# Keys and values of the prompt's latent attention: stored whole in memory and split by GpSimd when a head is fetched, values two heads at a time

## The chip, the cores and the metric

The kernel runs on one core of a Trainium2 chip. The metric is the device time of one execution in microseconds; the time of a kernel is the median of several executions. The profile shows one execution: what each engine did and when, and the clock that TensorE was granted (1.00 is its upper level of 2.4 GHz, 0.50 its lower level of 1.2 GHz).

The engines are TensorE (PE; its weight loads are PEld), VectorE (DVE), ScalarE (ACT), GpSimd (POOL) and SyncE (SP), which issues most of the DMA transfers; GpSimd issues the others here.

## What is computed

The reference is one step of a streaming encoder with two layers, over 1024 tokens of a prompt and 128 of samples. Each layer projects the normalised input, runs three mixers (a latent attention, a differential attention, a recurrence), gates them and merges them. The change concerns the latent attention of the prompt:

```python
c_q = rms_norm(c_q, lp['mla_q_norm'])
q = jnp.einsum('btr,rn->btn', c_q, lp['mla_w_uq']).reshape(B, T, MLA_HEADS, MLA_NOPE + MLA_ROPE)
...
c_kv = rms_norm(c_kv, lp['mla_kv_norm'])
...
q_lat = jnp.einsum('bthd,chd->bthc', q_nope, lp['mla_w_uk'])
...
s = jnp.einsum('bthc,bsc->bhts', ql, ckv_all) + jnp.einsum('bthr,bsr->bhts', qr, krope_all)
s = jnp.where(chunk_visible(qp, k_pos)[None, None], s.astype(jnp.float32) * mla_scale, NEG_INF)
p = jax.nn.softmax(s, axis=-1).astype(ckv_all.dtype)
return jnp.einsum('bhts,bsc->bthc', p, ckv_all)
```

There are 8 heads; a head has 64 features without position, 32 with rotary position, and values 64 wide. For the prompt the kernel does it the other way about: it expands the latents to keys and values of every head, 512 numbers of each per token.

## The kernel before, in words

A product of two float32 matrices is made of three matmuls (`mm3`, L196 to L202): each operand is split into a high part (a cast to a shorter form) and a low part (the rest), and high·high, high·low and low·high are added in PSUM. `split` (L191) makes the two parts of a tile: ScalarE casts the high part (L193), VectorE subtracts it for the low part (L194).

`layer` runs its stages one after the other: the differential attention, `c_phase`, `mla`, `mla_s` (the samples), the merge. Through all of them runs a queue of **filler tasks**, `z_task` and `gate_task`: products that depend on nothing but the layer's input. A task loads 512 KB of weights (`gs`, one buffer; SyncE, L236), ScalarE casts them (`gh`, L237), GpSimd makes the low part (`gl`, L240, four instructions). Then come three groups of 24 matmuls of 128x384 into `z` or `pg`; ScalarE takes the tanh of each group into a buffer `th` (four of them, L637 and L662), and SyncE stores `th` to `z` or `ts` (L646, L663). A credit in microseconds says how much filler stands between the matmuls of a stage; a burst of it, `BURST[4]`, stands before head 0's scores. A scheduler orders each engine's instructions once, when the program is built, and an engine works strictly in that order.

`c_phase` (L374) projects and normalises the latents, then makes three kinds of features and stores them: queries (`qn`, `qr`), keys (`keys`, L406: 128 features by up to 384 tokens at a time, into `kn`) and values (`vals`, L417: 128 tokens at a time, into `vm`). Each result is split on its way from PSUM into a tile `f` that holds both parts (`half`, `FB` = 6 buffers), and SyncE stores the tile, so that memory holds high and low parts side by side.

`mla` (L938) takes the heads in turn. `head(h)` fetches a head by four DMAs that GpSimd issues: `kT<-kn` (L957), `qT<-qn` (L958), `qT<-qr` (L959), `V<-vm` (L960). There are two buffers each of `kT`, `qT` and `V`, and head h uses `kT` and `qT` number h mod 2, so a fetch for head h waits until the scores of head h-2 are made. A unit is a head and a quarter of its queries. `scores` makes a unit's products into `sc` or `scm`; `soft` takes the maximum on VectorE (L811, L813) and the exponential on ScalarE into `P` (L821); two units later `pv` transposes `P` (L838), splits it into `ph` and `pl`, multiplies with `V` (L845 to L864), and `halves` (L876, L877) puts the sum into `ot`. At the end `rows_out` transposes the reciprocals of the row sums and stores them.

`mla_s` (L1018) begins with the samples' queries: GpSimd clears a part of `qrp` (L1024) and issues `qTh<-qn` and `qTl<-qn` (L1035); TensorE transposes `uk` into `ut` (L1047) and multiplies with `qTh` and `qTl` into `qlt`. Everything further in `mla_s` follows from `qlt`.

Of the kernel before, what the change touches and what calls it, by code (L numbers as in the profile page):

```python
# [9 lines left out]
F32 = mybir.dt.float32  # L10
# [4 lines left out]
ALU = mybir.AluOpType  # L15
# [3 lines left out]
DM, SEQ, NB, TS, PAST = 1024, 1024, 8, 16, 512  # L19
T = SEQ + NB * TS  # L20
NT = T // 128
NPT = SEQ // 128
EPS = 1e-6
NEG = -1e30
H = 8
QR, KR, NOPE, ROPE, VD = 256, 128, 64, 32, 64
# [12 lines left out]
def rr(ap):  # L39
    return ap.bitcast(F32)  # L40


class Net:
# [8 lines left out]
    TAIL = ((2, 0), (2, 1), (2, 2), (3, 0), (3, 1), (2, 3), (3, 2), (2, 4), (3, 3), (2, 5), (3, 4), (2, 6), (3, 5), (2, 7), (3, 6), (3, 7), (2, 8), (3, 8))  # L52
    GROUPS = (1, 3, 5, 7, 8)
    NORM = (0, 0)
    FB = 6
    CE = (1, 2, 1, 1)
    PVY = ((2, 1), (3, 1))
    TURNED = (1, 2)
# [202 lines left out]
    def setup(self):  # L261
        nc, ctx = self.nc, self.ctx
        i = self.i
        self.cp = ctx.enter_context(self.tc.tile_pool(name="cp", bufs=1))
        self.small = ctx.enter_context(self.tc.tile_pool(name="small", bufs=6))
        self.mmp = ctx.enter_context(self.tc.tile_pool(name="mmp", bufs=2, space=PSUM))
        self.ptp = ctx.enter_context(self.tc.tile_pool(name="ptp", bufs=2, space=PSUM))
        self.pop = ctx.enter_context(self.tc.tile_pool(name="pop", bufs=1, space=PSUM))
        self.scp = ctx.enter_context(self.tc.tile_pool(name="scp", bufs=3, space=PSUM))
        c = self.cp  # L270
        self.ident = c.tile([128, 128], F32, name="ident")
        nc.sync.dma_start(self.ident, i["k_ident"])
        self.identr = c.tile([128, 128], F32R, name="identr")
        nc.vector.tensor_copy(self.identr, self.ident)
        self.ones = c.tile([128, 2], F32, name="ones")
        nc.vector.memset(self.ones, 1.0)
        self.e2 = c.tile([128, 2], F32, name="e2")
        self.xpool = ctx.enter_context(self.tc.tile_pool(name="xpool", bufs=1))
        self.xh = self.xpool.tile([128, 8, T], F32R, name="xh")
        self.xl = self.xpool.tile([128, 8, T], F32R, name="xl")  # L280
        dt = self.tc.dram_tile
        ls = range(self.depth)
        self.qn = [dt([H * NOPE, 2, T], F32, name=f"qn{l}") for l in ls]
        self.qr = [dt([H * ROPE, 2, T], F32, name=f"qr{l}") for l in ls]
        self.kn = [dt([H * NOPE, 2, SEQ], F32, name=f"kn{l}") for l in ls]
        self.kr = [dt([ROPE, 2, T], F32, name=f"kr{l}") for l in ls]
        self.vm = [dt([H, 128, NPT, 2, VD], F32, name=f"vm{l}") for l in ls]
        self.qf, self.kf = ([[dt([512, T], F32, name=f"{k}{l}{x}") for x in "hl"] for l in ls] for k in ("qf", "kf"))
        if self.only == "debug":
            self.ob = [[self.o[f"ob{l}_{b}"] for b in range(3)] for l in range(self.depth)]  # L290
        else:
            self.ob = [[dt([512, T], F32, name=f"ob{l}_{b}") for b in range(3)] for l in range(self.depth)]
        self.zscr = [[dt([512, T], F32, name=f"z{l}_{b}") for b in range(2)] for l in range(self.depth)]
        self.hscr = [dt([LW, T], F32, name=f"hscr{l}") for l in range(self.depth)]
        self.rscr = [[dt([8, T], F32, name=f"rs{l}_{b}") for b in range(2)] for l in range(self.depth)]
        self.tscr = {(l, b): dt([DM, T], F32, name=f"ts{l}_{b}") for l in range(self.depth) for b in self.SPILL}
        self.xscr = dt([T, DM], F32, name="xscr")
# [76 lines left out]
    def c_phase(self, l):  # L374

        nc, i, o = self.nc, self.i, self.o
# [5 lines left out]
        with self.pool("cph") as p, ExitStack() as ea:  # L382
# [17 lines left out]
            def half():  # L400
                return pb.tile([128, 2, 384], F32R, tag="f", name="f", bufs=self.FB)

            def spill(dst, row, n, t0, x, tn=384):
                nc.sync.dma_start(dst[l][row : row + n, :, t0 : t0 + tn], rr(x[:n, :, :tn]))

            def keys(t0, tn):  # L406

                for b in range(4):
                    ps = self.sc()[:, :tn]
                    bs, ts = slice(b * 128, b * 128 + 128), slice(t0, t0 + tn)  # L410
                    self.mm3(ps, [(kvh[:, 0, bs], kvl[:, 0, bs], self.ckTh[:, ts], self.ckTl[:, ts])])
                    x = half()
                    self.split(ps, x[:, 0, :tn], x[:, 1, :tn])
                    spill(self.kn, b * 128, 128, t0, x, tn)
                    yield 0.5

            def vals(t):  # L417

                ps = self.sc()
                ts = slice(t * 128, t * 128 + 128)  # L420
                self.mm3(ps, [(self.ckTh[:, ts], self.ckTl[:, ts], kvh[:, 1], kvl[:, 1])])
                for g in range(2):
                    x = half().rearrange("p x t -> p (x t)")[:, :512].rearrange("p (h x v) -> p h x v", h=4, x=2)
                    self.split(ps[:, g * 256 : g * 256 + 256].rearrange("p (h v) -> p h v", h=4), x[:, :, 0], x[:, :, 1])
                    nc.sync.dma_start(self.vm[l][g * 4 : g * 4 + 4, :, t].rearrange("h p x v -> p h (x v)"), rr(x).rearrange("p h x v -> p h (x v)"))
                yield 0.65

            def project(t, raws):
# [46 lines left out]
            pb = ea.enter_context(self.pool("cpb"))  # L475
# [5 lines left out]
            for k in range(2):  # L481
                sv = st[:, k].rearrange("p (h d) -> p h d", d=96)
                for d0, d1, c0 in ((0, 64, 0), (64, 96, 512)):
                    hv, lv = (x[:, k, c0 : c0 + 8 * (d1 - d0)].rearrange("p (h d) -> p h d", h=8) for x in (uh, ul))
# [12 lines left out]
            for t in range(NT):  # L497
                ps = self.sc()[:, :256]
# [7 lines left out]
                c, t0 = t // 3, (t - 2) * 128  # L506

                for b in range(4):
                    ps = self.sc()[:, :384]
                    yield from self.proj_n(ps, t0, 384, uh, ul, kch=2, n0=b * 128, xh=cqh, xl=cql)  # L510
                    x = half()
# [3 lines left out]
                for b in range(2):  # L515
                    ps = self.pt("qrt")[:, :384]
                    for k in range(3):
                        nc.tensor.transpose(ps[:, k * 128 : k * 128 + 128], qs[k][:, b * 4 : b * 4 + 4].rearrange("p h r -> p (h r)"), self.ident)
                    x = half()
# [3 lines left out]
                ps = self.pt("krt")[:, :384]  # L523
                for k in range(3):
                    nc.tensor.transpose(ps[:32, k * 128 : k * 128 + 128], krn[:, t - 2 + k], self.ident)
                x = half()
                self.split(ps[:32], x[:32, 0], x[:32, 1])
                pn = min(SEQ - t0, 384)
                spill(self.kr, 0, ROPE, t0, x)
                yield  # L530
                yield from keys(t0, pn)
                for k in range(t - 2, min(t + 1, NPT)):
                    yield from vals(k)
# [404 lines left out]
    def mla(self, l):  # L938
        nc, i = self.nc, self.i
        with self.pool("mla") as p:  # L940
# [2 lines left out]
            nc.vector.memset(mask[0:64, 448:512], NEG)  # L943
            lsum = p.tile([128, NPT, H, 2], F32, name="lsum")
            nc.vector.memset(lsum, 0.0)
            ops, Ps = {}, {}
            kTs, qTs = ([p.tile([128, 2, SEQ], F32R, name=f"{x}T{k}") for k in range(2)] for x in "kq")
            for kT in kTs:
                nc.gpsimd.dma_start(kT[64:96], self.kr[l][:, :, :SEQ])
# [3 lines left out]
            def head(h):  # L953

                kT, qT = kTs[h % 2], qTs[h % 2]
                V = p.tile([128, NPT, 2 * VD], F32R, tag="V", name="V", bufs=2)
                nc.gpsimd.dma_start(kT[:64], self.kn[l][h * 64 : h * 64 + 64])  # L957
                nc.gpsimd.dma_start(qT[:64], self.qn[l][h * 64 : h * 64 + 64, :, :SEQ])  # L958
                nc.gpsimd.dma_start(qT[64:96], self.qr[l][h * 32 : h * 32 + 32, :, :SEQ])  # L959
                nc.gpsimd.dma_start(V, self.vm[l][h].rearrange("p t x v -> p t (x v)"))  # L960
                ops[h] = qT, kT, V
                yield

# [21 lines left out]
            def values(u):  # L985
# [11 lines left out]
                yield  # L997

            self.pipeline([(h, g) for h in range(H) for g in range(4)], lambda u: (u[0], lambda: head(u[0])), prep, scores, values, 4, self.BURST[4], self.LAG[1], (lambda u: (2 * (2 + (u[1] > 1)), self.pv_steps(1, u[1]))) if self.SPREAD[1] else None, self.WIDE)
            rl = p.tile([128, NPT * H], F32, name="rlm")  # L1000
            nc.vector.tensor_reduce(rl, lsum.rearrange("p i h k -> p (i h) k"), axis=AX.X, op=ALU.add)
            nc.vector.reciprocal(rl, rl)
            self.rows_out(p, rl, NPT, self.rscr[l][0], 0)

    def rows_out(self, p, r, nt, dst, t0):

        nc = self.nc
        for k0 in range(0, nt, 2):
            m = min(2, nt - k0)
            ps = self.pt("rst")  # L1010
            for t in range(m):
                nc.tensor.transpose(ps[:8, t * 128 : t * 128 + 128], r[:, (k0 + t) * 8 : (k0 + t) * 8 + 8], self.ident)
            ro = p.tile([8, 256], F32, tag="ro", name="ro", bufs=1)
            nc.scalar.copy(ro[:, : m * 128], ps[:8, : m * 128])
            nc.sync.dma_start(dst[:, t0 + k0 * 128 : t0 + (k0 + m) * 128], ro[:, : m * 128])

# [707 lines left out]
```

## Time and profile before

| | us |
|---|---|
| median of 3 runs | 3026.06 (3023.16 to 3031.2) |
| the profiled execution's own time | 3023.51 |
| its span in the trace | 3021.6 |
| TensorE busy in the span | 2857.7 (95%) |
| VectorE, ScalarE, GpSimd busy | 1651.7, 1395.0, 772.8 |
| bytes read and written in memory | 265.89 MB and 127.66 MB |
| `c_phase` of layer 0, its dense part | 886 to 934 |
| scores of `mla`, layer 0 | 957 to 1099 |
| mean granted clock | 0.987 |

Times in the rows further down are microseconds from the span's start. "Busy" leaves out register, branch, semaphore and DMA-issuing instructions. An engine's idle time is put down to what released it: `[3.58 <-ACT th L662]` reads: idle for 3.58 us, until ScalarE's write of `th` on line 662 was done. The time of an execution and its span differ by what lies before and behind the traced instructions (here 1.9 us).

### The profile page before, as it was taken

To read this page: it belongs to the slowest core of one execution; us is meant where nothing else is said; L and a number is where in the kernel's file an instruction comes from. 1 tells how busy PE (TensorE), PEld (TensorE's weight loads), DVE (VectorE), ACT (ScalarE), POOL (GpSimd) and SP (SyncE) were. 2 spreads that over 40 slices of the span, in tenths; PEclk is the share of its full clock that TensorE was granted. 3 is DMA by queue.
4 is the path that set the end of the run, shared out by engine and by line. 5 is a ranking of instruction groups with operands and counts; after the bars stand their busy time and mean duration, and the time that the engine had idled before them with its cause. 6 is when DMAs were issued, how large, how long until landed. Compare 5 with 4: busy or idle time off the path is not lost. (4 is left out here: it accounts for less than half of the span.)

```text
span 3021.6 us, 50750 instructions
## 1 busy us (share of the span) xinstructions
PE 2857.7 (95%) x18466; PEld 2705.9 (90%) x18466; DVE 1651.7 (55%) x3947; ACT 1395.0 (46%) x3367; POOL 772.8 (26%) x1132
## 2 busy tenths in 40 slices
PE   7999999999998999999989999999999989999998
PEld 7899899999897888999989998999999978889998
DVE  6322878747255855555343328777561557545543
ACT  4433766646333765312234347666452447542121
POOL 2221335120102113352131313342101111133620
PEclk9999999999999999999999999999999999999999
DMA  5434545265248533764133345452642584427541
GB/s 168 129 98 106 125 111 140 69 180 164 75 124 246 123 81 84 220 184 162 63 116 125 92 116 126 113 142 64 190 141 79 161 215 119 95 76 231 171 156 73
DMA packets 387658, 396.89 MB, mean 131 GB/s; under 512 B 56192, under 2 KB 342496, under 8 KB 386344
## 3 DMA queue, kind: packets, MB, share of 16 engines
q1 hardware_dynamic: 368048, 331.70, 36.7%
q0 software_dynamic: 19360, 61.95, 9.2%
q8 instruction: 146, 2.39, 0.3%
q14 instruction: 104, 0.85, 0.1%
HBM read 265.89 MB, written 127.66 MB: 130 GB/s over the span
## 5 line engine op out<-in xcount | busy, mean ns | idle before, releaser
L200 PE MATMUL pg<-xh,gh 128*128 128x384 f32 x1152 | 401.2, 348 | 7.5 <-ACT th L662 7.5
L821 ACT ACTIVATE P<-sc,mx 128x384 f32<-128x384 f32 (+4 forms) x598 | 335.5, 566 | 130.7 <-DVE mx L811 100.2
L201 PE MATMUL pg<-xl,gh 128*128 128x384 f32 x1152 | 395.8, 344 | 0.0
L202 PE MATMUL pg<-xh,gl 128*128 128x384 f32 x1152 | 395.3, 343 | 0.0
L240 POOL TENSOR_TENSOR gl<-gs,gh 128x256 fp32r<-128x256 f32 x288 | 230.3, 829 | 585.8 <-ACT gh L237 527.3
L194 DVE TENSOR_TENSOR pl<-pt,ph 128x512 fp32r<-128x512 f32 (+1 forms) x320 | 199.6, 634 | 53.2 <-ACT ph L193 50.8
L200 PEld LDWEIGHTS pg<-xh,gh 128*128 128x128 f32 x1152 | 218.2, 189 | 11.4 <-ACT th L662 9.2
L201 PEld LDWEIGHTS pg<-xl,gh 128*128 128x128 f32 x1152 | 218.1, 189 | 2.7
L202 PEld LDWEIGHTS pg<-xh,gl 128*128 128x128 f32 x1152 | 218.1, 189 | 0.9
L193 ACT CAST ph<-pt 128x512 fp32r<-128x512 f32 (+1 forms) x320 | 169.5, 544 | 81.8 <-PE pt L845 80.1
L200 PE MATMUL z<-xh,gh 128*128 128x384 f32 x576 | 203.3, 353 | 0.0
L201 PE MATMUL z<-xl,gh 128*128 128x384 f32 x576 | 199.6, 346 | 0.0
L202 PE MATMUL z<-xh,gl 128*128 128x384 f32 x576 | 198.4, 344 | 0.0
L200 PE MATMUL sc<-wyh,xh 128*128 128x256 f32 x576 | 163.0, 283 | 5.8 <-DVE xt L1550 5.8
L200 PE MATMUL dp<-wh,xh 128*128 128x256 f32 x576 | 165.2, 287 | 3.4 <-ACT e L575 2.1
L201 PE MATMUL dp<-wl,xh 128*128 128x256 f32 x576 | 164.4, 285 | 0.8 <-POOL wl L555 0.8
L202 PE MATMUL dp<-wh,xl 128*128 128x256 f32 x576 | 164.3, 285 | 0.0
L202 PE MATMUL sc<-wyh,ml 128*128 128x256 f32 x576 | 162.9, 283 | 0.0
L201 PE MATMUL sc<-wyl,xh 128*128 128x256 f32 x576 | 162.9, 283 | 0.0
L1235 PE MATMUL sc<-kT,qT 98*128 98x384 f32 (+3 forms) x384 | 140.6, 375 | 5.2 <-ACT P L821 4.6
L240 POOL TENSOR_TENSOR wol<-wos,woh 128x128 fp32r<-128x128 f32 x192 | 101.0, 554 | 172.2 <-ACT woh L237 153.6
L813 DVE TENSOR_REDUCE mx<-sc 128x1 f32<-128x384 f32 (+2 forms) x200 | 116.0, 586 | 39.1 <-PE sc L202 21.0
(456 smaller groups left out, 8355.3 us busy)
## 6 DMA issues: line engine op xcount, KB each, us to landing
gs<-in_w_in_dram SPq DMA_DIRECT2D x72, 512.0 KB
ts<-th SPq DMA_DIRECT2D x144, 192.0 KB
th<-ts SPq DMA_DIRECT2D x144, 192.0 KB
K<-in_cache_diff_k_dram SPq DMA_DIRECT2D x64, 256.0 KB
Vt<-in_cache_diff_v_dram SPq DMA_DIRECT2D x32, 512.0 KB
u<-ob SPq DMA_DIRECT2D x48, 288.0 KB
ws<-in_w_in_dram SPq DMA_DIRECT2D x24, 512.0 KB
z<-th SPq DMA_DIRECT2D x48, 192.0 KB
```

The source lines that it names most:

```text
L193: nc.scalar.copy(hi, src)
L194: (lo_engine or nc.vector).tensor_tensor(lo, src, rr(hi), op=ALU.subtract)
L200: nc.tensor.matmul(out, ah, bh, start=start and k == 0, stop=False)
L201: nc.tensor.matmul(out, ah, bl, start=False, stop=False)
L202: nc.tensor.matmul(out, al, bh, start=False, stop=stop and k == n - 1)
L240: (lo_engine or nc.gpsimd).tensor_tensor(lo[:, k : k + half], st[:, k : k + half], rr(hi[:, k : k + half]), op=ALU.subtract)
L813: nc.vector.tensor_reduce(mx, sc[:, : n1 - n0], axis=AX.X, op=ALU.max, negate=True)
L821: nc.scalar.activation(P[:, n0:n1], scs[k][:, : n1 - n0], AF.Exp, bias=mx, scale=1.0 if adds[k] is None else -1.0, accum_out=l2[:, k : k + 1])
L1235: nc.tensor.matmul(ps, lhs, kT[:, m, n0:n1], start=True, stop=True)
```

## The change

`kn` and `vm` hold whole float32 numbers, half the bytes. In `c_phase` a key tile and a value tile are copied from PSUM by one instruction, on ScalarE and VectorE by turns, into buffers of their own, `kx` (three) and `vx` (two); a value tile is stored by one DMA in place of two. `f` is left to the queries and the rotary keys and has 4 buffers. In `mla`, `head(h)` fetches the whole keys into a tile `kx` (one buffer), and every other head the whole values of two heads into `vx` (one buffer). In a second step the two parts are made from them: on GpSimd, a copy and a subtraction each for keys and values, and for head 0 on ScalarE and VectorE by `split`. `rows_out` uses two buffers under another name.

```diff
-    FB = 6
+    FB = 4
...
-        self.kn = [dt([H * NOPE, 2, SEQ], F32, name=f"kn{l}") for l in ls]
+        self.kn = [dt([H * NOPE, SEQ], F32, name=f"kn{l}") for l in ls]
...
-        self.vm = [dt([H, 128, NPT, 2, VD], F32, name=f"vm{l}") for l in ls]
+        self.vm = [dt([SEQ, H * VD], F32, name=f"vm{l}") for l in ls]
...
-                    x = half()
-                    self.split(ps, x[:, 0, :tn], x[:, 1, :tn])
-                    spill(self.kn, b * 128, 128, t0, x, tn)
+                    x = pb.tile([128, 384], F32, tag="kx", name="kx", bufs=3)
+                    (nc.vector.tensor_copy if b % 2 else nc.scalar.copy)(x[:, :tn], ps)
+                    nc.sync.dma_start(self.kn[l][b * 128 : b * 128 + 128, ts], x[:, :tn])
...
-                for g in range(2):
-                    x = half().rearrange("p x t -> p (x t)")[:, :512].rearrange("p (h x v) -> p h x v", h=4, x=2)
-                    self.split(ps[:, g * 256 : g * 256 + 256].rearrange("p (h v) -> p h v", h=4), x[:, :, 0], x[:, :, 1])
-                    nc.sync.dma_start(self.vm[l][g * 4 : g * 4 + 4, :, t].rearrange("h p x v -> p h (x v)"), rr(x).rearrange("p h x v -> p h (x v)"))
+                x = pb.tile([128, 512], F32, tag="vx", name="vx", bufs=2)
+                (nc.vector.tensor_copy if t % 2 else nc.scalar.copy)(x, ps)
+                nc.sync.dma_start(self.vm[l][ts], x)
...
-                nc.gpsimd.dma_start(kT[:64], self.kn[l][h * 64 : h * 64 + 64])
+                kx = p.tile([64, SEQ], F32, tag="kx", name="kx", bufs=1)
+                nc.gpsimd.dma_start(kx, self.kn[l][h * 64 : h * 64 + 64])
                 nc.gpsimd.dma_start(qT[:64], self.qn[l][h * 64 : h * 64 + 64, :, :SEQ])
                 nc.gpsimd.dma_start(qT[64:96], self.qr[l][h * 32 : h * 32 + 32, :, :SEQ])
-                nc.gpsimd.dma_start(V, self.vm[l][h].rearrange("p t x v -> p t (x v)"))
+                if h % 2 == 0:
+                    vx[0] = p.tile([128, NPT, 2 * VD], F32, tag="vx", name="vx", bufs=1)
+                    nc.gpsimd.dma_start(vx[0], self.vm[l][:, h * 64 : h * 64 + 128].rearrange("(t p) v -> p t v", p=128))
+                yield
+
+                vs = vx[0][:, :, h % 2 * VD : h % 2 * VD + VD]
+                for src, hi, lo in ((kx, kT[:64, 0], kT[:64, 1]), (vs, V[:, :, :VD], V[:, :, VD:])):
+                    if h:
+                        nc.gpsimd.tensor_copy(hi, src)
+                        nc.gpsimd.tensor_tensor(lo, src, rr(hi), op=ALU.subtract)
+                    else:
+                        self.split(src, hi, lo)
                 ops[h] = qT, kT, V
...
-            self.rows_out(p, rl, NPT, self.rscr[l][0], 0)
+            self.rows_out(p, rl, NPT, self.rscr[l][0], 0, "hv", 2)
```

The scheduler's order moves with it, in three places. The first is GpSimd's order in the middle of the heads. Before, a head is four DMAs:

```order
L957 DMA kT_10477<-kn_91 64x2048
L958 DMA qT_10479<-qn_87 64x2x1024
L959 DMA qT_10479<-qr_89 32x2x1024
L960 DMA V<-vm_95 128x1024
L957 DMA kT_10477<-kn_91 64x2048
```

Now (a head of even number, then one of odd number, which fetches no values):

```order
L968 CAST kT_10424<-kx 64x1024
L969 TENSOR_TENSOR kT_10424<-kx,kT_10424 64x1024
L957 DMA kx<-kn_91 64x1024
L968 CAST V<-vx 128x8x64
L958 DMA qT_10427<-qn_87 64x2x1024
L969 TENSOR_TENSOR V<-vx,V 128x8x64
L959 DMA qT_10427<-qr_89 32x2x1024
L968 CAST kT_10425<-kx 64x1024
L969 TENSOR_TENSOR kT_10425<-kx,kT_10425 64x1024
```

The split of a head and the fetch of the next stand between one another: the fetch of `kx` comes behind the split of the keys, the fetches of the queries behind parts of the split of the values.

The second place is GpSimd's order from the last head into `mla_s`. Before (`qrp`, `qTh` and `qTl` are those of `mla_s`, `gl` is a filler task's):

```order
L960 DMA V<-vm_95 128x1024
L1024 MEMSET qrp 32x1024
L1035 DMA qTh<-qn_87 64x8x128
L1035 DMA qTl<-qn_87 64x8x128
L240 TENSOR_TENSOR gl<-gs,gh 128x256 x4
```

Now:

```order
L968 CAST V<-vx 128x8x64
L969 TENSOR_TENSOR V<-vx,V 128x8x64
L240 TENSOR_TENSOR gl<-gs,gh 128x256 x4
L1035 MEMSET qrp 32x1024
L1046 DMA qTh<-qn_87 64x8x128
L1046 DMA qTl<-qn_87 64x8x128
```

The four `gl`, which wait for ScalarE's `gh`, moved from behind the fetches for `mla_s` to ahead of them.

The third place is ScalarE's order at the entry to `mla`. Before (`gh` are filler weights, the `P` are head 0's first units):

```order
L662 ACTIVATE th<-pg 128x384
L237 CAST gh<-gs 128x1024
L662 ACTIVATE th<-pg 128x384 x2
L821 ACTIVATE P,lsum<-sc,mx 128x128
L821 ACTIVATE P,lsum<-sc,mx 128x256
L821 ACTIVATE P,lsum<-sc,mx 128x384
L237 CAST gh<-gs 128x1024
L821 ACTIVATE P,lsum<-sc,mx 128x512
```

Now:

```order
L237 CAST gh<-gs 128x1024
L636 ACTIVATE th<-z 128x384 x3
L237 CAST gh<-gs 128x1024
L636 ACTIVATE th<-z 128x384
L193 CAST kT_10424<-kx 64x1024
L661 ACTIVATE th<-pg 128x384 x2
L820 ACTIVATE P,lsum<-sc,mx 128x128
L193 CAST V<-vx 128x8x64
L820 ACTIVATE P,lsum<-sc,mx 128x256
L820 ACTIVATE P,lsum<-sc,mx 128x384
L820 ACTIVATE P,lsum<-sc,mx 128x512
```

The CAST of `gh` that stood ahead of the unit's last `P` is gone from this place (it stands among the `P` of head 1 now), and head 0's two CASTs stand ahead of its first and its second `P`. Lines of the changed kernel lie 1 lower from `c_phase` on, and 11 higher behind `head`.

## Rows read from the trace of the kernel before

**Rows 1.** The page: busy time, share of the span and instructions of each engine.

```profile
PE 2857.7 (95%) x18466; PEld 2705.9 (90%) x18466; DVE 1651.7 (55%) x3947; ACT 1395.0 (46%) x3367; POOL 772.8 (26%) x1132
```

**Rows 2.** Windows: stretch, its length, busy (count) per engine, clock, DMA share, GB/s.

```profile
886.00:934.00 48.00, 48.00 (x288) 45.13 (x287) 33.01 (x84) 24.01 (x57) 2.84 (x4) 1.00 0.92 304
934.00:957.00 23.00, 19.42 (x101) 18.97 (x100) 10.71 (x14) 4.46 (x10) 6.85 (x12) 0.93 0.98 269
957.00:979.00 22.00, 11.94 (x60) 10.08 (x59) 8.77 (x23) 10.01 (x29) 4.08 (x8) 0.77 0.60 137
979.00:1099.00 120.00, 112.97 (x772) 98.74 (x770) 95.82 (x234) 92.78 (x262) 13.75 (x25) 1.00 0.47 107
...
2436.00:2459.00 23.00, 19.60 (x104) 19.15 (x102) 10.62 (x14) 4.47 (x11) 7.24 (x13) 0.93 0.97 260
2459.00:2481.00 22.00, 11.52 (x58) 9.68 (x57) 8.70 (x23) 9.87 (x30) 3.73 (x7) 0.77 0.60 138
```

**Rows 3.** Waits, 880 to 1140 us: engine, line, releaser; total us, times, longest.

```profile
PE sc L200 <- ACT P L821: 9.2, 1, 9.2
...
PE pg L200 <- ACT th L662: 3.6, 1, 3.6
```

**Rows 4.** Timeline of ScalarE: start, us, instruction, idle time before it and releaser.

```profile
950.69 0.49 ACT L662 ACTIVATE th<-pg 128x384 f32<-128x384 f32 x1 [10.72 <-DMA z<-th]
...
969.07 1.04 ACT L237 CAST gh<-gs 128x1024 fp32r<-128x1024 f32 x1 [9.24 <-DMA gs<-in_w_in_dram]
...
1121.45 1.05 ACT L237 CAST gh<-gs 128x1024 fp32r<-128x1024 f32 x1 [2.23 <-PE pg L201]
```

**Rows 5.** DMA issues, 880 to 1100 us: count, KB each, median us to landing.

```profile
kT<-kn POOLq DMA_DIRECT2D x8, 512.0 KB, 6.8
...
V<-vm POOLq DMA_DIRECT2D x8, 512.0 KB, 4.9
...
qTh<-qn POOLq DMA_DIRECT2D x1, 256.0 KB, 4.2
```

**Rows 6.** GpSimd's groups by form: busy, mean ns, idle time before.

```profile
L240 POOL TENSOR_TENSOR gl<-gs,gh 128x256 fp32r<-128x256 f32 x288 | 230.3, 829 | 585.8 <-ACT gh L237 527.3 <-PE kst L1360 41.8 <-PE ckt L1086 16.6
...
L1216 POOL TENSOR_TENSOR V<-nat,V 128x512 fp32r<-128x512 f32 x16 | 20.6, 1285 | 21.1 <-ACT V L1215 21.0
```

**Rows 7.** Timeline of GpSimd in the heads.

```profile
977.99 2.82 POOL L240 TENSOR_TENSOR gl<-gs,gh 128x256 fp32r<-128x256 f32 x4
...
1010.80 0.57 POOL L960 DMA_DIRECT2D V<-vm  x1 [15.40 <-PE sc L202]
...
1028.27 0.57 POOL L960 DMA_DIRECT2D V<-vm  x1 [15.25 <-PE scm L202]
```

**Rows 8.** Timeline of GpSimd at the end of `mla`.

```profile
1098.71 0.95 POOL L1024 MEMSET qrp<- 32x1024 f32 x1 [17.01 <-PE sc L202]
1099.61 0.69 POOL L1035 DMA_DIRECT2D qTh<-qn  x1
...
1122.64 2.81 POOL L240 TENSOR_TENSOR gl<-gs,gh 128x256 fp32r<-128x256 f32 x4 [21.66 <-ACT gh L237]
```

**Rows 9.** Timeline of TensorE: the first `qlt` product.

```profile
1126.77 0.32 PE L200 MATMUL qlt<-qTh,uTh 64*128 64x128 f32 x1
```

**Rows 10.** Windows: a hole elsewhere in the span and the 3 us behind it.

```profile
1262.00:1266.00 4.00, 1.21 (x7) 0.92 (x7) 3.94 (x5) 0.62 (x1) 4.00 (x3) 0.97 0.73 215
1266.00:1269.00 3.00, 3.00 (x11) 3.00 (x10) 1.60 (x3) 0.67 (x1) 2.65 (x5) 0.50 0.26 71
```

**Rows 11.** Waits, 884 to 936 us: ScalarE for the stores from `f`.

```profile
ACT f L193 <- DMA qn<-f: 1.6, 3, 0.7
...
ACT f L193 <- DMA qr<-f: 1.0, 2, 0.6
```

**Rows 12.** Timeline of VectorE, beside the `gl` of rows 7.

```profile
979.52 1.18 DVE L194 TENSOR_TENSOR pl<-pt,ph 128x384 fp32r<-128x384 f32 x2 [1.22 <-ACT ph L193]
```

**Rows 13.** VectorE's group of that form over the whole span: busy, mean ns.

```profile
L194 DVE TENSOR_TENSOR pl<-pt,ph 128x384 fp32r<-128x384 f32 x128 | 70.7, 553 | 23.7 <-ACT ph L193 23.0
```

More of the change, by code (lines that the diff above doesn't have):

```diff
@@ L945, in mla @@
             nc.vector.memset(lsum, 0.0)
-            ops, Ps = {}, {}
+            ops, Ps, vx = {}, {}, [None]
             kTs, qTs = ([p.tile([128, 2, SEQ], F32R, name=f"{x}T{k}") for k in range(2)] for x in "kq")
@@ L1002, in mla, with rows_out @@
             nc.vector.reciprocal(rl, rl)
-            self.rows_out(p, rl, NPT, self.rscr[l][0], 0)
-    def rows_out(self, p, r, nt, dst, t0):
+            self.rows_out(p, rl, NPT, self.rscr[l][0], 0, "hv", 2)
+    def rows_out(self, p, r, nt, dst, t0, tag="ro", bufs=1):
         nc = self.nc
@@ L1012, in rows_out @@
                 nc.tensor.transpose(ps[:8, t * 128 : t * 128 + 128], r[:, (k0 + t) * 8 : (k0 + t) * 8 + 8], self.ident)
-            ro = p.tile([8, 256], F32, tag="ro", name="ro", bufs=1)
+            ro = p.tile([8, 256], F32, tag=tag, name="ro", bufs=bufs)
             nc.scalar.copy(ro[:, : m * 128], ps[:8, : m * 128])
```

## The prediction, made before the changed kernel ran

> **What bounds the kernel now.** The page's busy times come first: TensorE is busy for 95% of the span and no other engine for more than 55% [rows 1]. So an edit pays only where TensorE waits or runs slowly, and the next view is the table of windows around the code that changes [rows 2]. In `c_phase` (886 to 934 us) TensorE is busy for 48.00 of 48 us at full clock, while the DMA engines are busy for 0.92 of the time: they are nearly full, but nothing waits for them yet. The bill comes at the entry to `mla`. From 934 to 957 us TensorE lacks 3.58 us and its mean clock is 0.93; from 957 to 979 us it lacks 10.06 us at 0.77. Then the heads run well: 112.97 busy of 120 us at clock 1.00. Layer 1 shows the same at 2436 and 2459 us.
>
> The list of waits names the two holes: 3.6 us behind ScalarE's `th`, 9.2 us behind ScalarE's `P` [rows 3]. ScalarE's timeline tells what it stood on [rows 4]. At 950.69 us the tanh into `th` had waited 10.72 us for a buffer that the store `z<-th` had not yet read out, so here the full DMA engines reach TensorE. At 969.07 us a CAST for a filler task's weights (`gh`) had waited 9.24 us for its load, and the last `P` of head 0's first unit stood behind it in ScalarE's order. A hole costs more than its length, since the clock is at half speed after it: 0.07 of 19.42 busy us is 1.4 us, 0.23 of 11.94 is 2.7 us. Layer 0 loses 3.6 + 1.4 + 9.2 + 2.7 = 16.9 us. Layer 1, by its windows and with the same 0.86 us of small gaps taken off the second, loses 3.4 + 1.4 + 9.6 + 2.7 = 17.1 us. Together **34.0 us** can be won, 1.1% of the time.
>
> **The change part by part.** *Bytes.* The eight key fetches and eight value fetches of a layer are 512 KB each [rows 5], so `kn` and `vm` are 4.2 MB each, written and read. Halved, 4.2 MB fewer are written in a stretch that moves 304 GB/s: 13.8 us of transfer per layer. A backlog of about ten us at the end of `c_phase` is what held `z<-th` back, so the first hole (3.6 + 1.4) should close. It also lets the first heads' fetches land earlier, and in `mla`, where the DMA engines are busy for 0.47, it frees what nobody waits for.
>
> *Order at the entry.* By the order of instructions the CAST of `gh` that blocked `P` now stands some 20 instructions later, among those of head 1. So the second hole (9.2 + 2.7) should go too. In its place ScalarE and VectorE split head 0's keys and values: CAST `kT` stands ahead of two `th` and the first `P`, CAST `V` ahead of the second `P`. They wait for the fetches `kx` and `vx`, which wait for the stores of the last chunk. Counting matmuls, 141 of the filler stand between the last `vals` product and head 0's first scores; they were 95. At 48.00/288 = 0.17 to 0.18 us each that is about 25 us. The way from the last store through the fetches is two landings: with 6.8 us [rows 5] for a fetch and up to twice that in full queues, plus about 3 us for the two splits, I get 17 to 25 us. So it fits barely; I take 1 us per layer left over, between 0 and 5.
>
> *The split on GpSimd.* For each head from 1 on, four instructions: CAST and subtraction for 64x1024 of `kT`, and the same for 128x512 of `V`. Subtractions of 128x256 take 829 ns and of 128x512 1285 ns [rows 6], so 1.8 ns for a further element and 2.2 us for 1024. The two subtractions are 1.29 + 2.2 = 3.5 us. No row has a CAST of this size on GpSimd; between nothing and the subtractions' price, that is 0 to 3.5 us. It walks as many elements, so I take 2.8, nearer the upper end: 6.3 us per head (3.5 to 7.0). GpSimd has room: it issues four DMAs per head of 0.5 to 0.6 us and then stands idle for over 15 us of 17.5, as before the `V` fetch at 1010.80 us [rows 7]. A head's `kT` may be written when the scores of the head two before it are done, 17.5 us before it is needed; 6.3 us of split and some 2 us of issues end well within that. The fetch of queries now stands behind two CASTs and a subtraction, some 5 us later, with 10 us left to land. I cost the split at nothing. Its cover is this idle time; without it every head would be longer, which is a rival below. ScalarE and VectorE lose 16 instructions each per layer, off the path.
>
> *The end of `mla`.* Here the change adds a wait. Before, GpSimd cleared `qrp` and issued `qTh` and `qTl` at 1099.61 us, 27 us before the first `qlt` product that reads them; the four `gl` came at 1122.64 us [rows 8, 9]. Now the four `gl` stand ahead, and they wait for ScalarE's CAST of `gh` (1121.45 us in the trace [rows 4]). From that CAST's start t: the `gl` start at t+1.2 and end at t+4.0, the memset of 0.95 ends at t+4.95, `qTh` is issued there and lands 4.2 us later [rows 5], at t+9.15; `qTl` 0.7 us after. The product wants it at 1126.77 - 1121.45 = 5.3 us, and 5 more filler matmuls stand ahead of it now, so t+6.2. The hole is 2.9 us (to 3.6 if `qTl` counts). Behind the wait stand the two fetches alone, but the whole of `mla_s` follows from `qlt`. After a hole of 2.8 us elsewhere the clock is at half for 3 us [rows 10], 1.5 us lost. Sum 4.4 us per layer, **+8.8**; at least +5.8 without the clock, at most +10.2.
>
> *Buffers in `c_phase`.* With 4 `f` instead of 6, a buffer comes round sooner, but keys and values no longer use it. ScalarE already waits for stores from `f`: 1.6 us in three and 1.0 us in two [rows 11], and TensorE shows none of it. Bounds: 0 (TensorE's 48.00 of 48) to 6 us per layer (half of the 21 `f` tiles that are left, at 0.6). I take three waits of 0.7, **2 us** per layer, as the densest stretch keeps its order.
>
> Sum from the profiled execution's own 3023.5 us: -34.0 + 8.8 + 4 (`f`) + 2 (entry) = -19.2, so 3004.3 us. The median of the runs is 2.5 us above that execution; I say **3005 us**.
>
> **Rivals.** *The wait moves within `c_phase`* (3011 us). Four buffers and stores that stay near the DMA limit (0.92) give back 5 us per layer instead of 2. For it: `f` is already waited for. Against: fewer tiles share the buffers.
>
> *The entry hole is only halved* (3019 us). If the chain of store, fetch and split takes 25 us plus 7 (one further landing of 6.8), head 0's scores stand 7 us in each layer instead of 1, with a half clock of 1.4 behind: +15. For it: two landings in a row under a DMA share of 0.98. Against: 13.8 us fewer of transfer ahead of it. This is also how the change would look if halved bytes relieve nothing.
>
> *Nothing is lost at the end* (2993 us). If the CAST of `gh` comes earlier than the products need, the +8.8 falls away, and `f` costs 1.
>
> *GpSimd and VectorE hold each other up* (3043 us, slower). If each of GpSimd's splits keeps VectorE from working, VectorE's 95.82/120 x 17.5 = 14.0 us per head become 20.3, 2.8 over the head's 17.5: 14 heads make +39. It decides as soon as more than 3.5 us per head collide. Against: at 979.52 us VectorE made two subtractions in 1.18 us, beside the `gl` of 977.99 us that ran till 980.8: 0.59 us each, where the mean is 0.55 [rows 7, 12, 13]. The Trainium skill (SBUF — State Buffer, "SBUF: two separate sides") says that VectorE and GpSimd share a port pair as an exclusive lock, held for a whole instruction, when VectorE reads two SBUF operands. By that rule this case stays small, since those subtractions, and VectorE's other work in the heads, read one operand from PSUM; the trace agrees. The skill also advises against the move as such: in GPSIMD Engine Reference, "Engine selection", two-input elementwise work on GpSimd is put at about twice VectorE's time. By these rows it is 1.285 us for 512 columns against 0.55 us for 384, so about 1.75; it changes the sum only where GpSimd is waited for.
>
> **How the numbers follow.** My case has 0.48 (3000 to 3010), the `f` waits 0.15, the halved hole 0.19, nothing lost at the end 0.10, the collision 0.08. This kernel's measurement can tell about 0.3% or 9 us from no change: faster is below 3017, slower above 3035. So faster has 0.48 + 0.15 + 0.10 = 0.73, same 0.19, slower 0.08. The range goes from 2993 to 3022: it takes in all but the collision and the worse half of the halved hole.
>
> **What would show it.** Right: no hole behind `th` or `P` at the entry and clock 1.00 there; the fetches `kT<-kn` gone, `kx` of 256 KB; a hole of about 3 us ahead of `qlt`, with `qTh` issued behind four `gl`; heads still 17.5 us apart, GpSimd busy 6 to 9 us in each; DMA share in `c_phase` clearly under 0.92. Wrong: heads longer than 17.5 us; a wait for `kT` or `V` by the scores of any head after the first; a hole of several us at head 0; `f` waits on TensorE in `c_phase`.

## The result, and the profile after

The changed kernel takes 3012.25 us in the median (8 runs, 3005.64 to 3016.94), the kernel before 3024.61 us (8 runs, 3020.65 to 3031.2). The ratio is 0.9949 with a 95% interval of 0.9936 to 0.9961: 0.5% faster, some 15 us by the ratio and 12.4 us between these medians, where 3005 us was forecast with a range of 2993 to 3022. The time lies in the range, but 7 us above the figure and outside the main case's 3000 to 3010; the gain is two thirds to four fifths of the 19.2 us in the forecast's sum. The profiled execution took 3012.3 us with a span of 3010.5 us.

The page's busy times (columns as in [rows 1]):

```profile
PE 2862.9 (95%) x18466; PEld 2708.3 (90%) x18466; DVE 1650.8 (55%) x3915; ACT 1386.3 (46%) x3335; POOL 847.4 (28%) x1180
```

TensorE does the same matmuls and is busy for 5.2 us more than in [rows 1]: the span fell by 11.1 us, so its idle time fell by 16.3 us, and a part of that was given back at half clock. The table of windows says where (columns as in [rows 2]); here `mla` begins at about 955 us:

```profile
886.00:934.00 48.00, 47.51 (x282) 43.00 (x281) 31.12 (x74) 21.00 (x46) 2.48 (x5) 1.00 0.78 270
934.00:957.00 23.00, 21.87 (x125) 21.27 (x124) 12.84 (x18) 6.11 (x14) 11.57 (x17) 1.00 0.93 205
957.00:969.00 12.00, 11.51 (x66) 9.57 (x65) 7.82 (x22) 8.55 (x28) 7.33 (x7) 1.00 0.71 162
969.00:1089.00 120.00, 113.59 (x775) 98.85 (x774) 96.90 (x234) 94.18 (x262) 43.59 (x44) 1.00 0.31 76
...
1112.00:1119.00 7.00, 4.49 (x27) 3.88 (x25) 0.68 (x1) 1.07 (x2) 4.17 (x6) 0.98 0.87 222
1119.00:1133.00 14.00, 13.23 (x51) 12.37 (x52) 3.23 (x7) 2.75 (x5) 3.61 (x12) 0.52 0.51 103
1133.00:1140.00 7.00, 6.99 (x52) 6.35 (x49) 5.38 (x20) 4.33 (x13) 2.76 (x8) 1.00 0.48 114
```

The DMA share in `c_phase` fell from 0.92 to 0.78. At the entry TensorE now lacks 1.13 us of 23 and 0.49 of 12, at clock 1.00, where [rows 2] had 3.58 and 10.06 at 0.93 and 0.77. The heads run as before, with GpSimd busy for 43.59 us of 120 and no longer 13.75. And behind the heads stands a stretch that was not there: TensorE is busy for 13.23 of 14 us, but at clock 0.52, so that 51 matmuls fit where the 7 us behind it hold 52.

TensorE's waits from 880 to 1000 us, longest first, answer to [rows 3]; both of its rows are gone:

```profile
PE po L859 <- ACT ph L193: 1.4, 3, 0.6
PE pg L200 <- DVE th L638: 1.1, 1, 1.1
PE sc L200 <- ACT P L820: 0.5, 2, 0.2
```

The end of `mla` answers to [rows 8, 9]. GpSimd's timeline:

```profile
1111.04 2.82 POOL L240 TENSOR_TENSOR gl<-gs,gh 128x256 fp32r<-128x256 f32 x4 [39.39 <-ACT gh L237]
1113.92 0.95 POOL L1035 MEMSET qrp<- 32x1024 f32 x1
1114.82 0.73 POOL L1046 DMA_DIRECT2D qTh<-qn  x1
1115.54 0.68 POOL L1046 DMA_DIRECT2D qTl<-qn  x1
```

TensorE's timeline there, the first `qlt` product and the place where the clock came back:

```profile
1119.57 0.44 PE L200 MATMUL qlt<-qTh,uTh 64*128 64x128 f32 x1 [2.73 <-DMA qTh<-qn]
...
1131.91 0.52 PE L200 MATMUL pg<-xh,gh 128*128 128x384 f32 x1
1132.23 0.44 PE L201 MATMUL pg<-xl,gh 128*128 128x384 f32 x1
1132.50 0.34 PE L202 MATMUL pg<-xh,gl 128*128 128x384 f32 x1
```

GpSimd had stood idle for 39 us, waiting for `gh` with the fetches behind it. The hole is 2.73 us; a filler matmul takes 0.52 us and not 0.34 until 1132.2 us.

To price the places, count TensorE's matmuls (18466 in either trace) and compare the times at which each trace reaches the same count. From count 5400 to 6400 lies the entry of layer 0, from 6400 to 7200 the end of its `mla`; 14800, 15700 and 16600 bound the same places in layer 1. The changed kernel's two profiled executions (the first two rows) differ by up to 2 us at one place, so less than that says nothing. Microseconds gained (-) or lost (+) against the kernel before:

| kernel | entry 0 | end 0 | entry 1 | end 1 |
|---|---|---|---|---|
| changed | -14.3 | +8.0 | -15.3 | +8.2 |
| changed, once more (e10) | -16.3 | +7.7 | -15.6 | +8.3 |
| e1, `qTh` by SyncE | -16.0 | +0.3 | -15.3 | +2.7 |
| e3, stores twice | -8.2 | +8.5 | -5.5 | +8.4 |
| e5, fetches of before in bytes | -16.1 | +7.2 | -17.2 | +8.7 |
| e6, both | -6.6 | +7.7 | -5.6 | +8.5 |
| e9, before with later fetches | -6.8 | -0.1 | -7.3 | +0.3 |

The entries give 29.6 us, the ends take back 16.2.

### The profile page after: what moved, and what is told of

It reads as the page before. It is cut to its first block, busy times and chain, and to the rows that moved or that the text cites. A ratio compares the mean times of both kernels' runs of the same rounds, so it can differ in the third digit from the quotient of the medians.

```text
span 3010.5 us, 50598 instructions
## 1 busy us (share of the span) xinstructions
PE 2862.9 (95%) x18466; PEld 2708.3 (90%) x18466; DVE 1650.8 (55%) x3915; ACT 1386.3 (46%) x3335; POOL 847.4 (28%) x1180
## 5 line engine op out<-in xcount | busy, mean ns | idle before, releaser
L237 ACT CAST gh<-gs 128x1024 fp32r<-128x1024 f32 x72 | 75.7, 1052 | 120.4 <-DMA gs<-in_w_in_dram 37.9
```

Source lines behind the costliest of these rows:

```text
L237: nc.scalar.copy(hi, st)
```

## The experiments

The runs were made on chips on which the kernel before took 3030.9, 3030.5 and 3032.9 us in the median, more than the 3024.61 us above. So what is compared is the ratio to the kernel before on the same chip.

### e1 and e11: the fetches of `mla_s` out of GpSimd's queue

```diff
-                    nc.gpsimd.dma_start(qT[x], self.qn[l][:, x, SEQ:].rearrange("(h d) t -> d h t", h=H))
+                    nc.sync.dma_start(rr(qT[x]), self.qn[l][:, x, SEQ:].rearrange("(h d) t -> d h t", h=H))
```

> The changed kernel with qTh and qTl fetched by SyncE in place of GpSimd, so that they no longer stand behind the four gl; TensorE's order stays as in the changed kernel up to there. Theory A (at the end of mla the wait for the fetches costs a hole of 2.7 to 3.0 us and, behind it, some 6 us of half clock, 8 to 9 us in each layer): the hole is at most 1 us, the granted clock stays 1.00 behind it, and the time falls by 17 us, 12 to 19, to about 2995. Theory B (the hole alone costs; the clock falls there in any case, because of the narrow qlt products): the time falls by 6 us to about 3006 and the clock is still 0.5 for some 13 us behind the first qlt.

The ratio is 0.9909 (0.9891 to 0.9926). The changed kernel, 0.9949, is 0.0040 above it: 12 us, the lower end of theory A. Windows of e1 from 1115 us on, around its first `qlt` products:

```profile
1115.00:1122.00 7.00, 6.46 (x38) 5.81 (x37) 0.68 (x1) 2.15 (x4) 3.78 (x5) 1.00 0.68 159
1122.00:1136.00 14.00, 13.98 (x98) 12.96 (x98) 7.55 (x21) 7.28 (x18) 6.77 (x18) 1.00 0.71 170
```

and its first `qlt` product:

```profile
1121.59 0.29 PE L200 MATMUL qlt<-qTh,uTh 64*128 64x128 f32 x1 [0.35 <-DMA qTh<-qn]
```

The hole is 0.35 us, and the 14 us behind it hold 98 matmuls at clock 1.00 where the changed kernel's 14 us held 51 at 0.52. The same narrow products run, so in layer 0 they are not what brings the clock down (theory B falls there): the hole is. By the table the two ends cost 0.3 and 2.7 us now, so 13.2 us were won there. In layer 1 a window of 14 us behind the products still has clock 0.88, with no wait of TensorE over 1.1 us near it; why is open.

The same kernel again, with the changed kernel beside it:

> The version of e1 once more, beside the changed kernel on the same chip: by the 8.4 and 9.7 us that the two tails cost, less 1 us left in each, 0.004 to 0.006 below the changed kernel's ratio (theory A of e1); 0.002 or less below it if the clock's part of these were not to be won.

> The changed kernel as it is, once more, beside the two others of this call on one chip: the ratio to the kernel before stays within 0.9936 to 0.9961 if chips and days do not matter at this level.

e11's ratio is 0.9906 (0.9889 to 0.9922), e10's 0.9952 (0.9936 to 0.9969): 0.0046 apart, as theory A had it. This version beats both kernels, by 0.9% and 0.45%.

### e2: work in the hole

```diff
+                    if h4 == 0:
+                        dm = self.pt("dm")
+                        for k in range(26):
+                            nc.tensor.matmul(dm[:, :384], self.xh[:, k % 8, :128], self.xh[:, k % 8, :384], start=k == 0, stop=k == 25)
                     ps = self.pt("qlt")
```

> The changed kernel with 26 further matmuls of 128x384, whose result nobody reads, ahead of the first qlt product of each layer: 26 x 0.174 = 4.5 us of work per layer, and the fetches come as late as before. Theory A (the hole brings the clock down): no hole, clock 1.00 behind it, per layer +4.5 of work, -2.9 of hole, -6 of half clock: -4.4, so about 9 us less in all, near 3003. Theory B (the clock falls there in any case): +1.6 per layer, so 3 us more, near 3015, with the clock at 0.5 behind the qlt products.

The ratio is 0.9962 (0.9947 to 0.9976), 4 us above the changed kernel: theory B's number, but not its reason. TensorE's timeline:

```profile
1110.07 4.78 PE L1064 MATMUL dm<-xh 128*128 128x384 f32 x26
1115.14 0.29 PE L200 MATMUL qlt<-qTh,uTh 64*128 64x128 f32 x1 [0.29 <-DMA qTh<-qn]
1117.64 0.47 PE L201 MATMUL qlt<-qTl,uTh 64*128 64x128 f32 x1 [2.21 <-DMA qTl<-qn]
```

The scheduler also moved filler matmuls: 13 that stood ahead of the product with `qTl` in the changed kernel stand behind it now, so that TensorE met that second fetch 2.21 us early. A hole was left, and the clock fell behind it again. The run therefore does not separate the theories (e1 does); it shows that a hole of 2.2 us is enough here.

### e3: the bytes of the stores back

```diff
+                    nc.sync.dma_start(self.kn2[l][b * 128 : b * 128 + 128, ts], x[:, :tn])
                     nc.sync.dma_start(self.kn[l][b * 128 : b * 128 + 128, ts], x[:, :tn])
...
+                nc.sync.dma_start(self.vm2[l][ts], x)
                 nc.sync.dma_start(self.vm[l][ts], x)
```

> The changed kernel with each store of keys and values made twice, the second copy into a memory tensor that nobody reads: the writes of c_phase are as many bytes as before the change. The scheduler then puts the CAST of gh back ahead of head 0's last P. Theory A (the gain at the entry to mla comes from the bytes written in c_phase, through the store z<-th, the load gs and the order that follows from them): the holes come back, 20 to 34 us more than the changed kernel, 3032 to 3046. Theory B (the gain comes from the whole layout: fewer splits in c_phase, or GpSimd's splits): at most 5 us more.

The ratio is 1.0005 (0.999 to 1.002), 17 us above the changed kernel. That is 3 us short of theory A and far from B; what it shows is in the parts. Its waits from 880 to 1140 us:

```profile
ACT th L665 <- DMA z<-th: 9.2, 1, 9.2
PE qlt L200 <- DMA qTh<-qn: 3.0, 1, 3.0
...
PE pg L200 <- ACT th L665: 1.8, 1, 1.8
...
PE sc L200 <- ACT kT L193: 1.5, 1, 1.5
```

A hole is back behind `th` and `z<-th`, of 1.8 us where the kernel before had 3.6 (in layer 1 it is 2.9 of 3.4), and head 0's scores now wait for the split of their keys, 1.5 us for ScalarE's part and 0.9 for VectorE's, in both layers. The second hole is not back, though the CAST of `gh` stands ahead of head 0's last `P` again. ScalarE's timeline:

```profile
960.84 0.58 ACT L824 ACTIVATE P<-sc,mx 128x384 f32<-128x384 f32 x1 [0.83 <-DVE mx L814]
...
961.41 1.04 ACT L237 CAST gh<-gs 128x1024 fp32r<-128x1024 f32 x1
...
962.34 0.69 ACT L824 ACTIVATE P<-sc,mx 128x512 f32<-128x512 f32 x1
```

The CAST did not wait: its load was there. By the table the halved stores are worth 6.1 us at entry 0 and 9.8 at entry 1, and the other half of the gain has another cause. One thing stays together here: e3 makes 40 stores of keys and values in a layer, the changed kernel 20 and the kernel before 28, and SyncE issues them back to back until 941 us. So a part may be due to the number of stores and not to their bytes; no run separates the two.

### e5 and e6: the bytes of the fetches back

Each head but the last fetches 128 rows of `kn` (64 of them unused), and every head fetches `vx`; e6 adds the doubled stores of e3.

```diff
-                nc.gpsimd.dma_start(kx, self.kn[l][h * 64 : h * 64 + 64])
+                nc.gpsimd.dma_start(kw[:n], self.kn[l][h * 64 : h * 64 + n])
...
-                if h % 2 == 0:
+                if True:
```

> The changed kernel with the fetches of before in bytes: each head but the last fetches 128 rows of kn (512 KB, half of them not used), and each head fetches vx (512 KB). The order of ScalarE at the entry stays that of the changed kernel (the CAST of gh stands in head 1). Theory A (the long wait at the entry needed both: a load gs that lands late because it stands with head 1's fetches, and a P behind its CAST): no hole over 3 us at the entry, and the time within 4 us of the changed kernel. Theory B (the bytes that are read decide by themselves): 10 us more than the changed kernel.

> The stores made twice as in e3 and the fetches of before in bytes as in e5. The CAST of gh stands ahead of head 0's last P, as before the change. Theory A (second hole: the load gs shares the DMA engines with head 1's 1.75 MB of fetches): the CAST of gh waits for its load by 4 to 9 us again, P behind it, and a hole of that size stands at head 0's scores; with its half clock 6 to 11 us per layer more than e3, so 12 to 22 us over e3 and over the kernel before. Theory B (the order alone, or the split, made the hole): as e3, within 4 us.

e5's ratio is 0.9945 (0.9928 to 0.9963), the changed kernel's: the bytes read cost nothing (theory A). e6's is 1.002 (1.0006 to 1.0035), 4.6 us above e3 and not the 12 to 22 of theory A: the second hole stayed away with all the bytes of before. Theory A named the right collision, but put it down to the bytes; e6's queues show that here the load went first. SyncE's issue of the load, and ScalarE's CAST:

```profile
959.91 0.38 SPq L236 DMA_DIRECT2D gs<-in_w_in_dram  x1
```

```profile
965.40 1.03 ACT L237 CAST gh<-gs 128x1024 fp32r<-128x1024 f32 x1
```

and GpSimd's issue of head 1's keys:

```profile
961.94 0.59 POOL L963 DMA_DIRECT2D kx<-kn  x1 [3.86 <-DVE kT L194]
```

There is one buffer `kx`, so head 1's fetch waits until VectorE has split head 0's keys, and the load gets ahead of it by 2 us, in e3 as in e6. In the kernel before, head 1 had buffers of its own: its four fetches were issued from 956.20 us on, ahead of the load, and the load landed at 969.0 us [rows 4], 10.8 us after its issue. GpSimd's and SyncE's timelines there:

```profile
956.20 0.56 POOL L957 DMA_DIRECT2D kT<-kn  x1
...
957.87 0.56 POOL L960 DMA_DIRECT2D V<-vm  x1
```

```profile
958.23 0.38 SPq L236 DMA_DIRECT2D gs<-in_w_in_dram  x1
```

The changed kernel is a third case. GpSimd, SyncE and ScalarE there:

```profile
951.62 0.56 POOL L957 DMA_DIRECT2D kx<-kn  x1
```

```profile
954.32 0.38 SPq L236 DMA_DIRECT2D gs<-in_w_in_dram  x1
```

```profile
969.11 1.09 ACT L237 CAST gh<-gs 128x1024 fp32r<-128x1024 f32 x1
```

Head 1's fetches (1 MB, since the values are there already) are ahead of the load again, by 1.6 us and more. The load landed by 960 us, since the DMA share from 960 to 961 us is 0.01: at most 5.7 us after its issue. Its CAST stands among the `P` of head 1 and does not wait. In e5 it is the same: fetches from 950.95 to 952.13 us, the load at 953.63, the CAST at 967.44 without a wait. This fits theory A of e5, that the hole needs both a late load and a `P` behind its CAST: in e3 and e6 the first is missing, in the changed kernel and e5 the second. No run has a load as late as 10.8 us with its CAST behind the `P`.

### e9: the kernel before, with head 1's fetches held back

```diff
+                for x in ((kT[0:1, 0, 0:2], qT[0:1, 0, 0:2], qT[64:65, 0, 0:2], V[0:1, 0, 0:2]) if h == 1 else ()):
+                    nc.gpsimd.tensor_copy(x, lsum[0:1, 2, 0])
                 nc.gpsimd.dma_start(kT[:64], self.kn[l][h * 64 : h * 64 + 64])
```

> The kernel before, its stores and fetches as they are, but for one wait: GpSimd copies two numbers of the row sums that ScalarE writes with the first P of head 0's second unit into head 1's kT, qT and V ahead of head 1's fetches (which overwrite them), so that these 1.75 MB are issued some 3 us later, behind the load gs and not ahead of it. Theory A (the second hole of the kernel before came from that load sharing the DMA engines with head 1's fetches): the load lands in 5 to 7 us in place of 10.8, the CAST of gh waits 1 to 4 us in place of 9.2, the hole shrinks to at most 4 us, and the time falls by 10 to 24 us, ratio 0.992 to 0.997; the hole behind th (3.6 and 3.4 us) stays. Theory B (the load is late in any case while c_phase's stores drain): hole and time stay, ratio 0.998 to 1.002.

The ratio is 0.9946 (0.9926 to 0.9966): theory A. One wait in the kernel before is worth as much as the whole change. The load's issue, the CAST, and GpSimd's first fetch for head 1, each in its engine's timeline:

```profile
959.54 0.38 SPq L236 DMA_DIRECT2D gs<-in_w_in_dram  x1
```

```profile
963.60 1.04 ACT L237 CAST gh<-gs 128x1024 fp32r<-128x1024 f32 x1 [2.44 <-DMA gs<-in_w_in_dram]
```

```profile
961.94 0.57 POOL L959 DMA_DIRECT2D kT<-kn  x1
```

The load lands 4.1 us after its issue in place of 10.8. TensorE's waits from 880 to 1000 us:

```profile
PE pg L200 <- ACT th L662: 3.3, 1, 3.3
...
PE sc L200 <- ACT P L821: 2.4, 1, 2.4
```

The hole behind `P` is 2.4 us and no longer 9.2; the one behind `th` stays, as it should, since the stores of `c_phase` are those of before. By the table the two parts add up within its error: e9 wins 6.8 and 7.3 us by the later fetches, the halved stores 6.1 and 9.8 (e3 against the changed kernel), together 12.9 and 17.1 where the changed kernel has 14.3 and 15.3.

### e4: who splits

```diff
-                    if h:
+                    if False:
                         nc.gpsimd.tensor_copy(hi, src)
```

> The changed kernel with the splits of all heads made by ScalarE and VectorE, as for head 0, in place of GpSimd: 1.6 us more per head on ScalarE (13.6 to 15.3 of 17.3) and 1.9 to 2.5 on VectorE (14.0 to about 16.3). Theory A (TensorE is fed late as soon as these two come close to the head's length): 0.5 to 1 us per head, 7 to 14 us more, 3019 to 3026. Theory B (there is room on every engine, so it does not matter who splits): within 3 us of the changed kernel.

The ratio is 0.996 (0.9946 to 0.9975), 3.3 us above the changed kernel, with intervals that overlap: theory B's bound, or just over it. From count 5900 to 6700, within the heads, this kernel loses 0.4 us against the kernel before where the changed one wins 1.3. So GpSimd's part of the change is worth some 1.7 us in layer 0; the other engines had nearly as much room.

### e7 and e8: six buffers `f`

`FB = 6` in place of 4, in the changed kernel (e7) and in e1's version (e8).

> The changed kernel with 6 buffers f instead of 4, the rest as it is. Theory A (the prediction's term: 4 buffers cost 2 us per layer): 4 us less than the changed kernel. Theory B (the stores keep up, since keys and values no longer use f): within 2 us, and no wait of TensorE for f in either.

> The version of e1 (qTh and qTl fetched by SyncE) with 6 buffers f. From e1's ratio of 0.991 to the kernel before: Theory A (the two edits add up): 0.9895 to 0.991 of the kernel before, no hole ahead of qlt and clock 1.00 behind it in both layers. Theory B (6 buffers shift the order and a new wait comes): over 0.993.

e7's ratio is 0.9972 (0.996 to 0.9984), 7 us above the changed kernel; e8's is 0.9932 (0.9908 to 0.9956), 7 us above e1. Neither theory of e7 had that sign; e8 is theory B by its number. TensorE waits for no `f` in either e7 or the changed kernel. The scheduler orders some products of `c_phase` in another way, but no new wait of that size was found, and e7's entries are as good as the changed kernel's (-15.1 and -15.8 us by the count of matmuls). Why six buffers are no better, and perhaps worse, stays open. That four buffers cost 2 us per layer is not borne out.

## Why the prediction came out as it did

The direction held, and so did the steps that close the holes, the second of them as far as the traces tell; one size, at the end of `mla`, was wrong by a factor of three to four. Two slips in the sums changed little. The runs' median lay 2.5 us above the profiled execution, so the sum of 3004.3 makes 3006.8 us and not 3005. And two landings of up to twice 6.8 us and 3 us of splits make up to 30 us, not 25.

- **Entry, -34.0 with +2 left over and +4 for `f`: -28 forecast, -29.6 by the count.** Both holes went in both layers. The step on bytes held for the first: with the stores doubled, the wait for `z<-th` and a hole came back (e3). The step on order fits the changed kernel's trace: the load is still issued behind head 1's fetches, and nothing waits, because its CAST stands later. No run tries this order alone in the kernel before, and the load is less late now: by 960 us as against a `P` that begins at 957.93, a CAST in the old place would have waited some 2 us, by my estimate from these two times. What the forecast left open is why the load was late. It was head 1's 1.75 MB of fetches, issued just ahead of it; holding them back in the kernel before (e9) took 6.8 of the hole's 9.2 us with the order as it was. The sentence that smaller fetches free what nobody waits for is too simple: a load of the filler stood behind them. But their bytes alone are worth nothing here (e5).
- **Head 0's split in time** held: 1 us per layer was allowed, and TensorE lacks 0.49 of 12 us around the first scores of layer 0. In layer 1 it waits for `P` by 1.6 us (below). With the stores doubled the split came 2.4 us late (e3).
- **The split at no cost** held. The four instructions are rows of the changed kernel now (groups by form):

```profile
L969 POOL TENSOR_TENSOR kT<-kx,kT 64x1024 fp32r<-64x1024 f32 x14 | 33.8, 2416 | 0.8
L969 POOL TENSOR_TENSOR V<-vx,V 128x512 fp32r<-128x512 f32 x14 | 18.4, 1313 | 0.5
L968 POOL CAST kT<-kx 64x1024 fp32r<-64x1024 f32 x14 | 14.8, 1056 | 3.9 <-DMA kx<-kn 3.9
...
L968 POOL CAST V<-vx 128x512 fp32r<-128x512 f32 x14 | 8.5, 609 | 111.9 <-PE po L863 111.9
```

  They sum to 5.4 us per head, within the 3.5 to 7.0 and under the 6.3 taken: a CAST costs under half of a subtraction, not four fifths.
- **The end of `mla`, +8.8 forecast, +16.2 by the count.** This is the step that failed, in its second term. The chain from the CAST of `gh` gave a hole of 2.9 us; it is 2.73 us, and 3.0 us with a further 1.2 for `qTl` in layer 1. But "the clock is at half for 3 us [rows 10], 1.5 us lost" was taken from another place. Here the clock stayed at half from 1119.6 to 1132.2 us in layer 0, 12.6 us, and in layer 1 filler matmuls take 0.52 us until about 2624 us, 9.4 us behind the second hole: about 6.3 and 4.7 us lost. TensorE's timeline in layer 1:

```profile
2614.57 0.47 PE L201 MATMUL qlt<-qTl,uTh 64*128 64x128 f32 x1 [1.18 <-DMA qTl<-qn]
...
2623.66 0.52 PE L200 MATMUL pg<-xh,gh 128*128 128x384 f32 x1
```

  One row of half clock from one other place was no bound for this one. The kernel before has a stretch of 10.3 us at half clock at the entry itself, which would have given some 5 us in place of 1.5 (columns as in [rows 2]):

```profile
965.40:975.70 10.30, 4.85 (x13) 4.00 (x14) 2.27 (x5) 4.58 (x13) 0.00 (x0) 0.50 0.20 55
```

- **`f`, +4 forecast:** not seen; see e7.
- **The rivals.** The wait within `c_phase` did not come. The entry hole went whole. The end was not free: the CAST of `gh` was as late as forecast. GpSimd and VectorE met only at head 0 (below); heads did not grow. The measured time lies nearest to the first rival's 3011 us; that is chance, since the excess comes from the end of `mla` and not from `c_phase`.

## What to carry to other kernels

A hole in TensorE is priced as its length plus the half clock behind it, and that second part must be bounded by the longest such stretch in the trace (10.3 us here, and 12.6 came), not by a handy one (3 us). When a load lands late, look at what was issued in the few microseconds ahead of it on every queue: moving 1.75 MB of prefetch behind the one urgent load gained here, alone, as much as the whole change. And when a change lengthens an engine's queue, read which small transfers now stand behind an instruction that waits: two fetches on another queue were worth 0.45%.

## What was not expected of the hardware

At head 0 of layer 1 VectorE subtracts for `V` with both operands in SBUF while GpSimd splits head 1. GpSimd's timeline in the changed kernel:

```profile
2446.20 2.39 POOL L969 TENSOR_TENSOR kT<-kx,kT 64x1024 fp32r<-64x1024 f32 x1
2448.56 1.70 POOL L969 TENSOR_TENSOR V<-vx,V 128x512 fp32r<-128x512 f32 x1
```

and VectorE's:

```profile
2446.91 2.22 DVE L194 TENSOR_TENSOR V<-vx,V 128x512 fp32r<-128x512 f32 x1
```

Elsewhere in the span VectorE's subtractions of that size on tiles in SBUF take 0.69 us each (groups by form):

```profile
L194 DVE TENSOR_TENSOR V<-Vt,V 128x512 fp32r<-128x512 f32 x64 | 42.1, 687 | 4.5 <-ACT V L193 4.2
```

Here it takes 2.22 us (2.43 in the changed kernel's second profile, e10); it ends at 2449.13 us, 0.54 us after GpSimd's first ends. GpSimd's next takes 1.70 us in place of its mean of 1.313. Each seems to have waited for the other to end. The Trainium skill (SBUF — State Buffer, "SBUF: two separate sides") describes this as an exclusive lock on a shared port pair, taken by VectorE when it reads two SBUF operands; these rows agree. It was not free: the row maximum that VectorE makes next came late, and TensorE's scores waited for ScalarE's `P` (waits from 2380 to 2500 us):

```profile
PE sc L200 <- ACT P L820: 1.6, 2, 1.4
```

In layer 0 the same subtraction takes 1.09 us, and TensorE waits for `P` by 0.5 us in all. Among VectorE's instructions in `mla` only the subtractions for head 0, two in each layer, read two operands in SBUF; its other work in the heads reads PSUM. That is why the collision rival stayed small. How large it would be in a kernel whose VectorE reads two SBUF operands all the time, no run here shows.

The other surprise is the clock's slow return: 12.6 us at the lower level with TensorE busy for 13.23 of 14 us, behind a hole of 2.73 us, while the 3.58 us hole of [rows 2] cost 1.4 us. In the changed kernel's second profile (e10) it was 9.1 us, behind holes of 2.67 and 1.34 us. What makes it long or short is open.
